# Layer norm sums beside the convolution: partial sums on POOL, a per-token shift as first summand, half the column sums on PE

## The chip, the cores and the metric

The kernel runs on one core of a Trainium2 chip. The metric is device time in microseconds (us) for one execution of the whole program. The core has five engines with their own instruction queues: PE (matmuls), DVE and POOL (elementwise vector work), ACT (activation functions, copies) and SP (here only the issue of DMAs). Each engine takes its instructions strictly in the order in which the program's scheduler put them.

## What is computed

One encoder block over 512 tokens of width 1024. The part that the change touches is the convolution branch and its neighbour, the attention:

```python
def conformer_conv(a_in, dw_w, dw_b, ln_g, ln_b, w_pw):
    u = a_in[..., :CONV_DIM] * jax.nn.sigmoid(a_in[..., CONV_DIM:])      # GLU
    u = lax.conv_general_dilated(u, dw_w[:, None, :], ...,               # 31 taps, one filter per channel
        feature_group_count=CONV_DIM) + dw_b
    u = layernorm(u, ln_g, ln_b)       # mean and variance over the 1024 channels of each token
    u = jax.nn.silu(u)
    return u @ w_pw
...
attn_out = windowed_gqa(q, k, v, attn_sink[l]) @ attn_w_o[l]             # 16 heads, band of 128 keys each way
merged = gates[:, :, 0, :] * conv_out + gates[:, :, 1, :] * attn_out     # sigmoid gates
x = x + merged @ w_out[l]
x = x + peer_ffn(rmsnorm(x, norm2_g[l]), ...)                            # 128 x 128 experts, 8 heads, top 16
```

The layer norm is (u - mean) * rsqrt(var + eps) * g + b over channels. Adding the same number to all channels of a token changes neither u - mean nor the variance.

## The kernel before

Activations are kept transposed: channels on the 128 partitions, 512 tokens along the free dimension, eight tiles of 128x512 for 1024 channels (`cv[:, k, :]`, k = 0 to 7). Every large matmul is done in three passes over split operands (`mm3`, L63 to L67): a value is split into a rounded part `hi` (ACT copy, L59) and the rest `lo` (a subtraction on POOL or DVE, L60). A projection (`proj`) of eight 128x128 weight chunks is therefore 24 matmuls of 512 columns; its weights come by DMA into `wraw`, are split in two halves (`whi` on ACT, `wlo` on the engine that `lo_engine` names), and there are four buffers of halves of each kind.

A scheduler lays out each engine's queue ahead of time: ready work goes in order of the program text, and work that stands later in the text fills an engine that has nothing earlier that is ready. Real durations don't change that order any more.

The stages around the change, in the order of the text:

1. **Convolution stage.** PE runs projections without a break: the GLU inputs (`glu`, two projections for each channel tile), keys, values, queries and 11 of the 16 gate projections (`fill`). Beside it DVE runs the 31 taps of the depthwise convolution (`conv`, L258 to L267) for pairs of channel tiles, the taps of the two tiles interleaved. The first tap of a tile is a `tensor_scalar` (L263) that writes the accumulator `ca` in PSUM with the bias `dwb` added; the other 30 are `scalar_tensor_tensor` (L266), and the last one writes `cv` in SBUF. A pair needs the GLU results `ub` (L255) of its two tiles. POOL makes `wlo` for all projections.
2. **Attention.** 16 blocks `attend(g, b)` for four key heads g and four query blocks b; the PSUM banks for its outputs (`pso`) are those that the convolution's accumulators held. ACT does the exponentials (L336, L338), half of the scaling (L344) and the copies `ph`, `qh` (L59); DVE the masked logits (L328), the other half and the rests `pl`, `ql` (L60). Five gate projections fill in between, each written by ACT into the gate tiles `sg` (L303).
3. **Layer norm.** Column sums over channels are matmuls with a matrix `ones` whose entries are 1/1024: eight of `cv` for the mean (L398), then, after DVE has subtracted the mean (L403) and ACT has squared (L405), eight of the squares for the variance (L406). These matmuls are of plain float32 and show as two passes of 512 columns each. Then ACT takes the square root (L408), DVE the reciprocal (L409), and per tile DVE multiplies (L411), ACT applies Silu (L413), and the result is split into `ac_hi`, `ac_lo` for the pointwise projection. These two take the buffers of the transposed input `hT`, whose last reader is the last gate projection.
4. **Output projections.** The two gates' sigmoids are two ACT instructions over 128x4096 (L421). Then eight projections with `w_o` (their `lo_engine` is DVE, L425), each result multiplied into the gate (L426), which frees the PSUM bank (there are two, `mm`); then eight with `w_pw`, then `w_out`. Weights of `w_out` are split with POOL (`olo`).
5. The expert stage, some three quarters of the time, which the change doesn't touch.

## Time and profile before

| | us |
|---|---|
| median of three runs | 1776.07 |
| lowest, highest | 1769.18, 1780.47 |
| the profiled execution | 1779.59 |
| its span on the core, first to last instruction | 1777.8 |

The profiled execution is 3.5 us above the median. The profile lists for each engine the time in which it was busy. Matmuls are pipelined and the listed durations of neighbours overlap, so a PE that is busy for the whole of a stretch may still be slower than its pace; the starts of successive matmuls show the pace. "[x <-E t Lnn]" at the end of a row of the timeline means that the engine had been idle for x us, and that the wait ended with engine E finishing a piece of work on tile t in line nn. PEclk is the share of full speed that TensorE's clock was granted.

### The profile page before, as it was taken

Reading aid. Unit: us, or ns where it says so; the run is one execution under the profiler, and the core shown is the slowest. Engines: PE = TensorE matmul, PEld = TensorE weight load, DVE = VectorE, ACT = ScalarE, POOL = GpSimd, SP = SyncE. Lnnn points to the kernel's source line nnn. Section 1 sums busy time; section 2 is a strip of 40 time slices with the busy share of each in tenths; the row PEclk is TensorE's granted clock in tenths of the full one; section 3 lists DMA queues with packets and bytes.
Section 4 is the critical chain, followed back from the end, with each engine's and each line's share of the span. In section 5 each row is a group of like instructions: output and inputs, shape, how many; then the busy total and the mean of one; then the engine's idle time right before and its main releaser. Section 6 shows DMA issues by size and latency. Waiting matters only on the chain.

```text
span 1777.8 us, 25338 instructions
## 1 busy us (share of the span) xinstructions
PE 1723.7 (97%) x8843; PEld 1487.6 (84%) x8843; DVE 1425.5 (80%) x2523; ACT 777.7 (44%) x1386; POOL 945.5 (53%) x745
## 2 busy tenths in 40 slices
PE   7999999989999979999999999999999999998998
PEld 6888876668888878998999999999999988997786
DVE  7999967674437999999668888888878768898964
ACT  5333368972253336665433333333433332332343
POOL 6544420020135444445358888878876677786401
PEclk9999999999999989999999999999999999999999
DMA  4232210043243125987879998988997888899952
GB/s 160 98 102 97 95 39 33 13 148 101 83 149 105 45 65 162 285 259 245 311 256 312 328 317 307 328 320 316 319 326 278 314 303 294 304 329 333 357 204 93
DMA packets 158976, 379.44 MB, mean 213 GB/s; under 512 B 12592, under 2 KB 64832, under 8 KB 158848
## 3 DMA queue, kind: packets, MB, share of 16 engines
q1 hardware_dynamic: 120720, 241.73, 38.9%
q0 software_dynamic: 37120, 134.52, 22.0%
q10 hardware_dynamic: 1008, 1.58, 0.3%
q8 instruction: 69, 1.13, 0.3%
q14 instruction: 59, 0.48, 0.1%
HBM read 346.84 MB, written 30.93 MB: 212 GB/s over the span
## 4 chain that ended last, share of the span: by engine, by line
PE 63%; DVE 13%; DMA 12%; issue 6%; POOL 3%; ACT 2%; SPq 0%; ACTq 0%; POOLq 0%; DVEq 0%
PE mm L65 7%; PE mm L67 7%; PE mm L66 7%; PE acc L67 6%; PE acc L66 6%; PE acc L65 6%; PE hps L66 6%; PE hps L65 6%; PE hps L67 5%; DMA row<-in_v_dram,eidx 5%; DMA uraw<-in_ut_dram 3%; DMA vraw<-in_v_dram 2%; PE s L65 2%; POOL row L701 1%; PE s L66 1%
## 5 line engine op out<-in xcount | busy, mean ns | idle before, releaser
L60 POOL TENSOR_TENSOR ulo<-uraw,uhi 128x512 fp32r<-128x512 f32 x256 | 400.7, 1581 | 306.6 <-ACT uhi L59 278.7
L67 PE MATMUL hps<-big,ulo 128*128 128x384 f32 x1024 | 349.0, 341 | 3.6 <-POOL ulo L60 3.6
L65 PE MATMUL hps<-big,uhi 128*128 128x384 f32 x1024 | 348.8, 341 | 2.2 <-ACT hb L504 2.1
L66 PE MATMUL hps<-big,uhi 128*128 128x384 f32 x1024 | 347.5, 339 | 0.0
L67 PE MATMUL acc<-vhl,pl 128*128 128x512 f32 x768 | 301.7, 393 | 8.0 <-DVE pl L60 8.0
L65 PE MATMUL acc<-vhl,ph 128*128 128x512 f32 x768 | 301.3, 392 | 3.6 <-ACT vhl L59 3.5
L66 PE MATMUL acc<-vhl,ph 128*128 128x512 f32 x768 | 301.7, 393 | 0.9 <-DVE vhl L60 0.9
L60 POOL TENSOR_TENSOR wlo<-wraw,whi 128x512 fp32r<-128x512 f32 x120 | 160.8, 1344 | 176.4 <-ACT whi L59 153.6
L708 DVE SCALAR_TENSOR_TENSOR row<-row,h2tok 128x1024 f32<-128x1024 f32 x128 | 206.0, 1610 | 58.3 <-DMA row<-in_u_dram,eidx 56.5
L719 DVE SCALAR_TENSOR_TENSOR yacc<-row,dots,yacc 128x1024 f32<-128x1024 f32 x127 | 193.3, 1522 | 58.4 <-DMA row<-in_v_dram,eidx 58.2
L59 ACT ACTIVATE vhl<-vraw 128x1024 fp32r<-128x1024 f32 x128 | 135.5, 1059 | 230.5 <-DMA vraw<-in_v_dram 207.8
L59 ACT ACTIVATE uhi<-uraw 128x512 fp32r<-128x512 f32 x256 | 157.1, 631 | 167.0 <-PE hps L66 75.3
L65 PEld LDWEIGHTS hps<-big,uhi 128*128 128x128 f32 x1024 | 194.4, 190 | 6.4 <-ACT hb L504 2.4
L67 PEld LDWEIGHTS hps<-big,ulo 128*128 128x128 f32 x1024 | 194.3, 190 | 5.3 <-POOL ulo L60 5.3
L66 PEld LDWEIGHTS hps<-big,uhi 128*128 128x128 f32 x1024 | 194.9, 190 | 4.0
L701 POOL DMA_INDIRECT row<-in_u_dram,eidx x128 | 178.6, 1396 | 31.6 <-issue 25.8
L59 ACT ACTIVATE whi<-wraw 128x512 fp32r<-128x512 f32 x152 | 95.2, 631 | 209.9 <-PE mm L66 141.5
L701 POOL DMA_INDIRECT row<-in_v_dram,eidx x128 | 155.1, 1211 | 55.5 <-DVE yacc L719 31.1
L60 DVE TENSOR_TENSOR vhl<-vraw,vhl 128x1024 fp32r<-128x1024 f32 x128 | 162.7, 1271 | 24.4 <-ACT vhl L59 24.2
L67 PEld LDWEIGHTS acc<-vhl,pl 128*128 128x128 f32 x768 | 145.3, 189 | 41.4 <-DVE pl L60 10.5
L65 PE MATMUL mm<-big,whi 128*128 128x512 f32 x448 | 178.0, 397 | 0.4 <-DVE big L105 0.4
L66 PE MATMUL mm<-big,whi 128*128 128x512 f32 x448 | 176.4, 394 | 0.0
(243 smaller groups left out, 3073.3 us busy)
## 6 DMA issues: line engine op xcount, KB each, us to landing
uraw<-in_ut_dram SPq DMA_DIRECT2D x128, 512.0 KB
vraw<-in_v_dram SPq DMA_DIRECT2D x128, 512.0 KB
gates_dram<-st SPq DMA_DIRECT2D x12, 2048.0 KB
gt<-gates_dram SPq DMA_DIRECT2D x96, 256.0 KB
wraw<-in_w_in_dram SPq DMA_DIRECT2D x42, 512.0 KB
wraw<-in_w_query_dram SPq DMA_DIRECT2D x16, 512.0 KB
wraw<-in_w_o_dram SPq DMA_DIRECT2D x8, 512.0 KB
oraw<-in_w_out_dram SPq DMA_DIRECT2D x16, 256.0 KB
```

The source lines that it names most:

```text
L59: ACT.activation(hi, src, AF.Copy)
L60: lo_engine.tensor_tensor(lo, src, f(hi), op=OP.subtract)
L65: PE.matmul(ps, wh, mh, start=first and i == 0, stop=False)
L66: PE.matmul(ps, wh, ml, start=False, stop=False)
L67: PE.matmul(ps, wl, mh, start=False, stop=last and i == n - 1)
L701: POOL.indirect_dma_start(out=row, out_offset=None, in_=table, in_offset=bass.IndirectOffsetOnAxis(ap=eidx[:, c:c + 1], axis=0))
L708: DVE.scalar_tensor_tensor(row, row, 1.0, h2tok, op0=OP.mult, op1=OP.mult, accum_out=dots[:, c:c + 1])
L719: DVE.scalar_tensor_tensor(yacc, row, dots[:, c:c + 1], yacc, op0=OP.mult, op1=OP.add)
```

## The change

Three things. First, the sums over channels for tiles 0 to 5 are made by POOL while the convolution still runs: `ssum` collects the sum of the tiles, `sqsum` that of their squares, so that only one partial sum and the last two tiles go through PE. Second, to keep the squares small, all tiles carry a per-token shift: the mean of tiles 0 and 1 (`cshift`, two matmuls, one ACT copy). POOL subtracts it from these two tiles; for tiles 2 to 7 an ACT instruction makes `dwb` minus `cshift`, and the first tap adds it (now a `scalar_tensor_tensor` too). The unused planes of the gate tiles `sg` hold these arrays. The variance is the mean of the squares less the square of the mean. Third, the sums are finished after the first attention block (`ln_sums`: six matmuls, four ACT instructions, one DVE subtraction), the square root stands right behind the attention loop, and the eight squares and the second pass over the tiles are gone. The `lo` halves of the `w_o` weights move from DVE to POOL (`proj` has POOL as its default).

```diff
@@ conv @@
+            cshift, ssum = sg[0][:, 6, :], sg[0][:, 7, :]
+            sqt, sqsum = sg[1][:, 6, :], sg[1][:, 7, :]
+
             def conv(pair, ubs):
                 accs = [psc.tile([P, S], F32, name="ca") for _ in pair]
+                offs = []
+                for i in pair:
+                    if i > 1:
+                        offs.append(accs[1] if i % 2 else sg[0][:, 5, :])
+                        ACT.activation(offs[-1], cshift, AF.Identity, scale=-1.0, bias=vec["dwb"][:, i:i + 1])
                 for j in range(TAPS):
-                    for i, ub, acc in zip(pair, ubs, accs):
-                        if j == 0:
+                    for n, (i, ub, acc) in enumerate(zip(pair, ubs, accs)):
+                        if j == 0 and i < 2:
                             DVE.tensor_scalar(acc, ub[:, :S], tapt[:, i, 0:1], vec["dwb"][:, i:i + 1],
                                               op0=OP.mult, op1=OP.add)
                         else:
                             DVE.scalar_tensor_tensor(cv[:, i, :] if j == TAPS - 1 else acc, ub[:, j:j + S],
-                                                     tapt[:, i, j:j + 1], acc, op0=OP.mult, op1=OP.add)
+                                                     tapt[:, i, j:j + 1], acc if j else offs[n],
+                                                     op0=OP.mult, op1=OP.add)
+                if pair[0] == 0:
+                    ps = psm.tile([P, S], F32, name="mm")
+                    for i in pair:
+                        PE.matmul(ps, ones, cv[:, i, :], start=i == 0, stop=i == 1)
+                    ACT.activation(cshift, ps, AF.Copy, scale=float(KD // 2))
+                    for i in pair:
+                        POOL.tensor_tensor(cv[:, i, :], cv[:, i, :], cshift, op=OP.subtract)
+                if pair[0] < KD - 2:
+                    for i in pair:
+                        if i == 1:
+                            POOL.tensor_tensor(ssum, cv[:, 0, :], cv[:, 1, :], op=OP.add)
+                        elif i:
+                            POOL.tensor_tensor(ssum, ssum, cv[:, i, :], op=OP.add)
+                        sq = sqt if i else sqsum
+                        POOL.tensor_tensor(sq, cv[:, i, :], cv[:, i, :], op=OP.mult)
+                        if i:
+                            POOL.tensor_tensor(sqsum, sqsum, sq, op=OP.add)
@@ attention and layer norm @@
+            lnp = ac.enter_context(tc.tile_pool(name="lnp", bufs=2))
+            mu = lnp.tile([P, S], F32, name="mu", bufs=1)
+            rs = lnp.tile([P, S], F32, name="rs", bufs=1)
+
+            def ln_sums():
+                ps = pso.tile([P, S], F32, name="ln")
+                for n, a in enumerate((ssum, cv[:, KD - 2, :], cv[:, KD - 1, :])):
+                    PE.matmul(ps, ones, a, start=n == 0, stop=n == 2)
+                ACT.activation(mu, ps, AF.Copy)
+                ACT.activation(rs, mu, AF.Square)
+                ps = pso.tile([P, S], F32, name="ln")
+                for n in range(2):
+                    sq = lnp.tile([P, S], F32, name="act", bufs=2)
+                    ACT.activation(sq, cv[:, KD - 2 + n, :], AF.Square)
+                    PE.matmul(ps, ones, sq, start=n == 0, stop=False)
+                PE.matmul(ps, ones, sqsum, start=False, stop=True)
+                DVE.tensor_tensor(rs, ps, rs, op=OP.subtract)
+
             for g in range(4):
                 make_bias(g)
                 for b in range(NT):
                     attend(g, b)
+                    if (g, b) == (0, 0):
+                        ln_sums()
                     if b == 1 or (g, b) == (0, 3):
                         fill(1)
-            lnp = ac.enter_context(tc.tile_pool(name="lnp", bufs=2))
             ac_hi, ac_lo = bigtile(), bigtile()
-            mu_ps = pso.tile([P, S], F32, name="ln")
-            for k in range(KD):
-                PE.matmul(mu_ps, ones, cv[:, k, :], start=k == 0, stop=k == KD - 1)
-            mu = lnp.tile([P, S], F32, name="rs", bufs=1)
-            ACT.activation(mu, mu_ps, AF.Copy)
-            var = pso.tile([P, S], F32, name="ln")
+            ACT.activation(rs, rs, AF.Sqrt, bias=epst)
+            DVE.reciprocal(rs, rs)
             for k in range(KD):
                 DVE.tensor_tensor(cv[:, k, :], cv[:, k, :], mu, op=OP.subtract)
-                sq = lnp.tile([P, S], F32, name="sq")
-                ACT.activation(sq, cv[:, k, :], AF.Square)
-                PE.matmul(var, ones, sq, start=k == 0, stop=k == KD - 1)
-            rs = lnp.tile([P, S], F32, name="rs", bufs=1)
-            ACT.activation(rs, var, AF.Sqrt, bias=epst)
-            DVE.reciprocal(rs, rs)
-            for k in range(KD):
                 DVE.tensor_tensor(cv[:, k, :], cv[:, k, :], rs, op=OP.mult)
                 act = lnp.tile([P, S], F32, name="act", bufs=2)
                 ACT.activation(act, cv[:, k, :], AF.Silu, scale=vec["lng"][:, k:k + 1],
@@ output projection @@
             for j in range(KD):
-                ps = proj(w_o[j], oT, lo_engine=DVE)
+                ps = proj(w_o[j], oT)
                 DVE.tensor_tensor(sg[1][:, j, :], ps, sg[1][:, j, :], op=OP.mult)
```

## Rows read from the trace of the kernel before

**Rows 1.** Windows, three stages: from:to, length, PE, PEld, DVE, ACT, POOL, PEclk, DMA.

```profile
45.00:231.00 186.00, 186.00 (x826) 153.55 (x825) 179.77 (x275) 59.86 (x104) 92.09 (x78) 1.00 0.30 98
231.00:367.00 136.00, 133.35 (x622) 92.96 (x620) 92.79 (x289) 113.66 (x274) 7.74 (x6) 1.00 0.07 22
367.00:418.00 51.00, 46.55 (x178) 35.07 (x178) 29.73 (x42) 28.13 (x44) 10.58 (x8) 0.93 0.53 174
```

**Rows 2.** Timeline of PE, 362 to 394 us: start, us, engine, line, tiles [idle before].

```profile
362.19 1.88 PE L406 MATMUL ln<-sq,ones 128*128 128x512 f32 x4
...
365.28 3.73 PE L406 MATMUL ln<-sq,ones 128*128 128x512 f32 x8
368.45 0.80 PE L65 MATMUL mm<-qh,whi 128*128 128x512 f32 x1
...
377.78 0.51 PE L65 MATMUL mm<-qh,whi 128*128 128x512 f32 x1 [1.43 <-DVE sg L426]
...
386.40 0.77 PE L65 MATMUL mm<-qh,whi 128*128 128x512 f32 x1 [2.76 <-DVE sg L426]
```

**Rows 3.** Timeline of DVE, 365 to 385 us, same columns.

```profile
366.31 0.69 DVE L60 TENSOR_TENSOR ql<-o,qh 64x512 fp32r<-64x512 f32 x1
...
373.65 3.35 DVE L409 RECIPROCAL rs<-rs 128x512 f32<-128x512 f32 x1 [4.72 <-ACT rs L408]
...
377.64 6.20 DVE L411 TENSOR_TENSOR cv<-cv,rs 128x512 f32<-128x512 f32 x7
```

**Rows 4.** Groups of PE's instructions, 367.5 to 418 us: count | busy, mean ns.

```profile
L65 PE MATMUL mm<-qh,whi 128*128 128x512 f32 x56 | 23.9, 427 | 4.2 <-DVE sg L426 4.2
```

**Rows 5.** The tile ln: duration min/median/max ns, first and last start.

```profile
L398 PE MATMUL ln<-cv,ones x16: 590/592/697, 317.2 to 333.6; 128*128 128x512 f32 x16
```

**Rows 6.** Timeline of ACT in the attention, two places.

```profile
307.86 1.28 ACT L421 ACT_TABLE_LOAD   x1
309.15 3.62 ACT L421 ACTIVATE sg<-sg 128x4096 f32<-128x4096 f32 x1
...
313.81 1.28 ACT L336 ACT_TABLE_LOAD   x1
...
358.12 0.58 ACT L400 ACTIVATE rs<-ln 128x512 f32<-128x512 f32 x1
```

**Rows 7.** Windows, PE's matmuls into attention output o alone: from:to, length, PE, PEclk.

```profile
262.00:278.00 16.00, 4.51 (x15) 1.00 0.11 34
...
306.00:322.00 16.00, 2.88 (x10) 1.00 0.04 14
322.00:338.00 16.00, 4.84 (x12) 1.00 0.10 34
```

**Rows 8.** Groups of instructions, 231 to 367 us, ACT.

```profile
L405 ACT ACTIVATE sq<-cv 128x512 f32<-128x512 f32 x5 | 2.9, 630 | 0.3 <-PE ln L406 0.3
```

**Rows 9.** Groups of instructions, 45 to 231 us, POOL and DVE.

```profile
L60 POOL TENSOR_TENSOR wlo<-wraw,whi 128x512 fp32r<-128x512 f32 x69 | 90.0, 1307 | 89.7 <-ACT whi L59 88.1 <-PE s L67 1.4
...
L266 DVE SCALAR_TENSOR_TENSOR ca<-ub,tapt,ca 128x512 f32<-128x512 f32 x232 | 154.7, 755 | 0.0
...
L255 DVE TENSOR_TENSOR ub<-mm,sgm 128x512 f32<-128x512 f32 x3 | 2.1, 688 | 2.8 <-ACT sgm L250 2.8
```

**Rows 10.** Timelines of POOL and DVE at the end of the first pair.

```profile
88.81 1.30 POOL L60 TENSOR_TENSOR wlo<-wraw,whi 128x512 fp32r<-128x512 f32 x1 [1.41 <-ACT whi L59]
91.20 0.11 POOL L252 MEMSET ub<- 128x15 f32 x1 [1.10 <-DVE cv L266]
...
91.70 0.58 DVE L364 SCALAR_TENSOR_TENSOR dist<-dist 128x384 f32<-128x384 f32 x1
...
94.46 1.49 DVE L366 TENSOR_TENSOR dist<-dist,L 128x384 f32<-128x384 f32 x1
```

**Rows 11.** Groups of instructions, 28 to 46 us, POOL and DVE.

```profile
L60 POOL TENSOR_TENSOR big<-cv,big 128x512 fp32r<-128x512 f32 x4 | 6.9, 1729 | 1.3 <-ACT big L59 1.3
...
L271 DVE SCALAR_TENSOR_TENSOR cv<-cv,g,sg 128x512 f32<-128x512 f32 x8 | 9.3, 1186 | 0.0
```

## Prediction

> **What bounds the kernel now.** I read the windows by stage first: beside each stretch stand its length and, engine by engine, busy time and count [rows 1]. In the convolution stage PE issues 826 matmuls in 186 us, one per 0.225 us, without a gap, and DVE is busy for 179.8 us of 186: two engines are full. In the attention PE is busy for 133.4 of 136 us, but with only 622 matmuls, many of them short, so that is no pace; ACT has 113.7 us of work in 136, the most of the others. From 367 to 418 us PE should be limited by itself, with 168 matmuls of `w_o` (three passes of 56) [rows 4], and isn't: it issues 178 in 51 us at a mean clock of 0.93 [rows 1].
>
> Why, PE's timeline shows [rows 2]. The last attention output is split when DVE ends `ql`, 366.31 + 0.69 = 367.0 us [rows 3]. But the variance's column sums hold PE until 368.45; four more of their passes follow among the projections (16 in all, as for the mean [rows 5], of which twelve stand in the two rows [rows 2]). Then PE idles 1.43 and 2.76 us for L426, the multiplication on DVE that frees the PSUM bank [rows 2]. DVE is late because the reciprocal (3.35 us, itself waiting 4.72 us for ACT's root) and seven multiplications (6.20 us) stand ahead of it [rows 3]. After the second gap the clock is granted at half: a mean of 0.93 over 51 us is 51 x 0.07 x 2 = 7.1 us at the lower level (1.2 instead of 2.4 GHz), which costs 3.6 us.
>
> **Tail: what is taken away.** Squares, their sums and the root's wait leave this stretch, and DVE is free for L426 at once. Term by term: 368.45 - 367.0 = 1.45; four passes at 1.88 / 4 = 0.47, less overlap 0.43, 1.7; the two gaps 4.2; the clock 3.6. Together -10.9 us. From the other end: 168 x 0.225 = 37.8 us from 367.0 is 404.8, against the end of the window that just holds them, 418 [rows 4]: -13. I take -10.9, with bounds -7 (one gap and its clock loss stay) and -13. The `lo` halves of `w_o` go to POOL at 1.31 instead of about 0.69 us on DVE: 2.6 us per projection of 24 x 0.225 = 5.4 us, beside the eight `olo`, and POOL is busy for 10.6 of 51 us there [rows 1, 9]; counted at nothing, as POOL has that room.
>
> **Convolution stage: what is added.** PE gets four passes, 4 x 0.43 = 1.7 us, in a stage where it has no gap. POOL gets six operations of 128x512 behind each of the first three pairs (two subtractions, one addition, two squares, one addition behind the first; two additions, two squares, two additions behind the others). At the 1.31 us of `wlo` that is 7.9 us in a row, and by the text they go before the `wlo` of the following projections, which POOL works off with half its time idle [rows 9]. How much lead has `wlo`? Four buffers of halves, 12 matmuls of 0.225 = 2.7 us for each: a half is begun when PE frees the one four back, so PE comes to it three halves (8.1 us) and two matmuls (0.45) later; ACT's copy (0.63, as for its other 128x512 work [rows 8]) and POOL's 1.30 [rows 10] leave 6.6 us. A row of 7.9 us makes one half late by 1.3 us and stalls PE by that. The two bursts near 92 and 142 us count, since the last GLU inputs come from PE behind them and DVE waits for such inputs already (up to 2.8 us [rows 9]); what PE loses there the last pair, and the attention behind it, gets later. So 1.7 + 2 x 1.3 = +4.3 us. Bounds: +1.7 if the scheduler puts `wlo` in between; +11.8 if POOL's operations take the 1.73 us that they take beside DVE work [rows 11], 2 x (10.4 - 6.6) = 7.6, and POOL stands 2.5 us for `cshift` with `wlo` behind it. The skew of the laid-out order is small: POOL's waits for the end of a pair are 1.10 us [rows 10].
>
> The new chain, last tap to sum (0.86) to ACT copy to ACT offset (0.63 each) to first tap, is about 2.5 us with its handovers; DVE has the distance tables (0.58, 1.49 [rows 10]) and a query split to do meanwhile, so nothing; uncovered 2.5 us. Later offsets are made while the other tile's tap runs: nothing, at most 0.6 us for each pair. Do POOL's added operations slow DVE? A tap takes 0.755 us on average over 232 with POOL busy for half the time [rows 9]: one input is in PSUM. The multiplication L271, with both inputs in SBUF, took 1.19 us on average beside POOL's `big` splits, and those 1.73 instead of 1.31 [rows 9, 11]. The Trainium skill says the same ("SBUF — State Buffer", Who interferes with whom): a DVE instruction with two SBUF inputs and a POOL instruction that reads SBUF exclude each other. By it the three first taps that read their offset from SBUF could each be held for one POOL operation, 3 x 1.3 = 3.9 us more. I count nothing for the taps.
>
> **Attention: what moves in.** ACT gets four instructions of 0.63 in `ln_sums` (2.5 us), and the root, which was behind the attention, can now run in the first gap of ACT after the first block. So can Silu for two tiles (two buffers `act`; the split that frees them needs `hT`'s buffers, which the last gate projection holds). What such an insertion costs the rows show for the sigmoids: each came into the attention with a table load before and one behind it, 1.28 each, 6.2 us with its 3.62 [rows 6]. The stretches of 16 us that hold them have 10 and 12 matmuls into `o` where an undisturbed one has 15 [rows 7]: 5.3 and 3.2 us of progress lost for 12.4 us of ACT, or 0.69. Root: 0.63 + 2 x 1.28 = 3.2. A pair of Silu: 1.3 + 2.6 = 3.9. Leaving: the mean's copy (0.58 [rows 6]) and five squares (2.9 [rows 8]). Net 2.5 + 3.2 + 3.9 - 3.5 = 6.1 us on ACT, times 0.69: +4.2 us. The reciprocal (3.35) and sixteen short DVE operations go into the 43 us that DVE has idle here [rows 1]; without that cover up to 3.4. PE's mean sums (16 passes [rows 5]) leave, twelve passes come: 1.7 us of filler less, nothing. Bounds: -2.4 (only the leaving counts) to +23 (below).
>
> The Trainium skill speaks against this order ("ScalarE: Activation LUTs", Table sets: the hidden batching unit): do all work of one table set before the next. It puts a switch at 2.66 us, load and drain; the sum with that for the four switches would be 4 x 1.38 x 0.69 = 3.8 us higher, 1778 us. The rows show the sigmoid starting 1.29 us behind its load's start [rows 6], no drain beyond, so the sum stays with 1.28.
>
> **Sum.** 4.3 + 4.2 - 10.9 = -2.4 us. The profiled execution, 1779.59 us, would become 1777.2; from the median, 3.5 us below it, 1776.07 - 2.4 = 1773.7. I forecast 1774 us: a real gain of 11 us at the tail, mostly spent ahead of it. 1% is 17.8 us, about what a measurement of this kernel can tell from no change.
>
> **Rivals.** *Clean gain.* The bursts slip between `wlo` (+1.7), the attention takes the insertions in gaps (-2.4), the tail gives 13: -13.7, 1762 us; if Silu pushes the second sigmoid behind the attention, 3.2 to 5.3 us more, 1757 to 1759. For it: ACT has 22 us idle in the attention; DVE sheds `wlo`. The mean's copy, ready when its sums ended near 334 us, ran only at 358.12 [rows 5, 6], so late work may simply stay late, and then adds no switches. Against: both sigmoids did get in.
>
> *Silu scattered through the attention (slower).* Place: ACT's gaps between exponentials, as soon as buffers allow. Eight single Silu with two loads each: 8 x (0.63 + 2.56) = 25.5; root 3.2, sums 2.5, eight `hi` copies 5.0, less 3.5: 32.7 us on ACT, times 0.69 is 22.6. With 4.3 - 10.9: +16, 1792 us; passed on in full, +26, 1802. It turns the gain into a loss when ACT gets 6.6 / 0.69 = 9.6 us, which is one more switch than I count, and passes 1% at 35. For it: the text puts Silu ahead of the sigmoids. Against: `hT` holds the buffers for six of them until the last gate projection, and ACT is 84% full (113.7 of 136).
>
> *POOL becomes the gate of the weights.* The upper bound of the convolution stage, +11.8, with the rest as summed: +5, 1781 us. For it: POOL then has 92 + 18 x 1.31 = 116 us of work in bursts. Against: half its time is idle.
>
> **How the numbers follow.** Forecast (1765 to 1783 us): 0.47. Clean gain: 0.29, about half of it beyond 1%. Scattered Silu: 0.14, most of it beyond 1%. POOL as gate: 0.10. So faster by over 1%: 0.15; slower by over 1%: 0.11; within: 0.74. The range leaves out the far ends of the clean gain and the full price of the scattered Silu: 1759 to 1790 us.
>
> **What would show it.** Tail: no column sums after 365 us, `w_o`'s 168 matmuls in 38 to 40 us, granted clock 1.00 there. Convolution: last tap 2 to 8 us later; six POOL operations in a row behind a pair, then a stall of PE of 1 to 2 us. Attention: two to four more table loads, stretch from last tap to last `ql` about 141 instead of 137 us. It is wrong if that stretch shortens, if loads number eight or more, or if PE stalls by over 5 us at a burst.

## The result, and the profile after

The changed kernel takes 1828.19 us (median of 4 runs, 1823.75 to 1839.05), the kernel before 1772.87 (4 runs, beside it): 1.031 times as long, 95% interval 1.027 to 1.035. That is +55.3 us where I had forecast -2.4; the time lies 38 us above the upper end of my range.

The waits of the changed kernel, 25 to 300 us (engine, line, tile, releaser: us in total, times, longest), name the place by the longest single waits (rows left out are marked):

```profile
...
ACT whi L59 <- PE mm L66: 56.8, 27, 2.2
PEld mm L280 <- DVE cv L274: 50.8, 2, 50.3
PE mm L280 <- DVE cv L274: 49.8, 1, 49.8
ACT sg L281 <- PE mm L280: 44.7, 1, 44.7
...
POOL ub L252 <- DVE cv L274: 39.7, 2, 39.2
...
```

And PE's timeline there (start, us; what idle time came before stands in brackets):

```profile
34.99 0.40 PE L66 MATMUL s<-ql,whi 128*128 128x512 f32 x1
35.23 0.40 PE L67 MATMUL s<-qh,wlo 128*128 128x512 f32 x1
85.45 3.78 PE L280 MATMUL mm<-cv,ones 128*128 128x512 f32 x4 [49.83 <-DVE cv L274]
...
89.46 0.63 PE L66 MATMUL mm<-ql,whi 128*128 128x512 f32 x1
89.89 0.63 PE L67 MATMUL mm<-qh,wlo 128*128 128x512 f32 x1
90.31 0.55 PE L65 MATMUL mm<-qh,whi 128*128 128x512 f32 x1
90.70 0.39 PE L66 MATMUL mm<-ql,whi 128*128 128x512 f32 x1
90.93 0.39 PE L67 MATMUL mm<-qh,wlo 128*128 128x512 f32 x1
```

L280 is the shift's column sum over the first two convolved tiles. It stands in PE's queue directly behind the second GLU projection (35 us), but its input, the last tap of the first pair, comes 50 us later. PE takes the queue as it stands: not one matmul ran in 49.83 us. The windows by stage (from:to, length; PE, PEld, DVE, ACT and POOL with counts; clock, DMA share, GB/s), against [rows 1]:

```profile
45.00:90.00 45.00, 4.54 (x7) 2.30 (x8) 41.06 (x63) 0.69 (x2) 1.61 (x6) 0.50 0.00 0
90.00:274.00 184.00, 184.00 (x814) 152.00 (x813) 144.51 (x209) 62.16 (x106) 106.73 (x88) 1.00 0.29 92
274.00:433.00 159.00, 149.58 (x646) 104.84 (x646) 105.20 (x303) 125.51 (x291) 14.15 (x11) 0.92 0.07 21
433.00:478.00 45.00, 43.78 (x187) 34.67 (x186) 9.57 (x13) 22.26 (x34) 29.52 (x23) 1.00 0.66 218
```

Seven matmuls in the first 45 us, where 826 in 186 us make some 200. Then 814 matmuls in 184 us, the old pace, to the last tap at 273.9 us; DVE, which was full before, is now busy for 144.5 of 184 us. The attention is longer too, and PE's clock in it 0.92. Only the tail shows what was forecast for it: 1.00 and no gaps to speak of, as the groups of `w_o`, 433 to 478 us, say against [rows 4]:

```profile
L67 PE MATMUL mm<-qh,wlo 128*128 128x512 f32 x62 | 24.6, 397 | 0.7 <-POOL wlo L60 0.7
L65 PE MATMUL mm<-qh,whi 128*128 128x512 f32 x62 | 24.6, 397 | 0.5 <-ACT whi L59 0.5
```

The table that carries the rest of this text has the milestones of every kernel run, read from the traces, in us: the end of the first pair's first tile on DVE, of the last tap, and of the last split `ql` of the attention; the stretch between the latter two; the start of `w_pw`, and the tail up to it; and how many matmuls of `w_o` were left when the attention ended. The experiments are described below.

| kernel | first tile | last tap | attention ends | stretch | `w_pw` starts | tail | left | ratio to before [interval] |
|---|---|---|---|---|---|---|---|---|
| before | 91.1 | 230.3 | 367.0 | 136.7 | 417.8 | 50.8 | 168 | |
| changed | 85.4 | 273.9 | 432.5 | 158.6 | 477.9 | 45.4 | 186 | 1.0306 [1.0267, 1.0345] |
| e1 sum in another bank | 92.1 | 233.8 | 384.3 | 150.5 | 428.9 | 44.6 | 185 | 1.0051 [1.0031, 1.0072] |
| e2 the sum alone | 85.5 | 273.1 | 422.0 | 148.9 | 474.4 | 52.4 | 168 | one run: 1830.6 |
| e3 `lo` on POOL alone | 90.8 | 230.0 | 369.7 | 139.7 | 422.4 | 52.7 | 168 | one run: 1777.5 |
| e4 no shift | 91.3 | 230.5 | 380.3 | 149.8 | 425.5 | 45.2 | 186 | one run: 1785.4 |
| e5 = e1, root held | 91.0 | 232.7 | 376.3 | 143.6 | 424.9 | 48.5 | 166 | 1.0046 [1.0020, 1.0073] |
| e6 = e5, `lo` on DVE | 91.0 | 232.7 | 376.3 | 143.6 | 422.6 | 46.3 | 166 | 1.0038 [1.0013, 1.0062] |
| e7 = e6, no shift | 92.2 | 231.9 | 376.3 | 144.4 | 422.4 | 46.1 | 166 | 1.0007 [0.9981, 1.0032] |
| e8 = e6, sums late | 90.7 | 232.3 | 369.1 | 136.8 | 415.8 | 46.7 | 167 | 0.9984 [0.9962, 1.0005] |
| e10 = e8, mult. on POOL | 90.8 | 232.5 | 370.8 | 138.3 | 417.0 | 46.2 | 167 | 0.9961 [0.9943, 0.9979] |
| e9 = e10, no shift | 92.6 | 232.2 | 368.9 | 136.7 | 415.1 | 46.2 | 167 | 0.9966 [0.9944, 0.9988] |
| e11 = e10, sums kept | 91.4 | 233.1 | 373.4 | 140.3 | 415.4 | 42.0 | 166 | 0.9985 [0.9965, 1.0005] |
| e12 = e11, no shift | 91.2 | 230.4 | 370.0 | 139.6 | 412.1 | 42.1 | 166 | 0.9951 [0.9933, 0.9968] |

From `w_pw` to the first matmul into `hps` (the next stage) all of them take 90 us; from there to the last matmul into `acc` 1250.6 to 1266.1 us, with no relation to the edits (before 1261.9, changed 1252.3). Each row of milestones is one execution, which can lie off its kernel's median (e1's by 13 us); the ratios are of medians, against runs of the kernel before in the same group (medians 1771.1 to 1776.1). The milestones up to `w_pw` therefore say more about the change than the last digit of the times; that the changed kernel is 60.1 us late at `w_pw` and 55.3 at the end is within this spread.

### The profile page after: what moved, and what is told of

It is laid out like the page before. It is cut to its first block, busy times and chain, and to the rows that moved or that the text cites. A ratio compares the mean times of both kernels' runs of the same rounds, so it can differ in the third digit from the quotient of the medians.

```text
span 1828.6 us, 25332 instructions
## 1 busy us (share of the span) xinstructions
PE 1725.1 (94%) x8827; PEld 1487.1 (81%) x8827; DVE 1422.1 (78%) x2508; ACT 788.4 (43%) x1393; POOL 975.2 (53%) x779
## 4 chain that ended last, share of the span: by engine, by line
PE 73%; DVE 13%; issue 7%; DMA 4%; POOL 1%; ACT 1%; ACTq 0%; POOLq 0%; SPq 0%; DVEq 0%
PE acc L66 8%; PE acc L67 8%; PE acc L65 8%; PE hps L65 8%; PE hps L66 8%; PE hps L67 8%; PE mm L65 6%; PE mm L66 6%; PE mm L67 6%; DVE ca L274 2%; DMA row<-in_v_dram,eidx 2%; DVE oij L707 1%; DVE ohl L709 1%; PE s L65 1%; POOL row L735 1%
## 5 line engine op out<-in xcount | busy, mean ns | idle before, releaser
L60 POOL TENSOR_TENSOR wlo<-wraw,whi 128x512 fp32r<-128x512 f32 x136 | 181.1, 1338 | 270.3 <-ACT whi L59 245.1
L742 DVE SCALAR_TENSOR_TENSOR row<-row,h2tok 128x1024 f32<-128x1024 f32 x128 | 188.4, 1472 | 59.8 <-DMA row<-in_u_dram,eidx 58.6
L753 DVE SCALAR_TENSOR_TENSOR yacc<-row,dots,yacc 128x1024 f32<-128x1024 f32 x127 | 187.1, 1474 | 44.4 <-DMA row<-in_v_dram,eidx 43.8
L59 ACT ACTIVATE ph<-hb 128x384 fp32r<-128x384 f32 (+1 forms) x132 | 67.3, 513 | 289.8 <-PE acc L66 282.6
L59 ACT ACTIVATE whi<-wraw 128x512 fp32r<-128x512 f32 x152 | 95.1, 629 | 208.9 <-PE mm L66 129.6
L735 POOL DMA_INDIRECT row<-in_u_dram,eidx x128 | 167.3, 1307 | 31.7 <-issue 25.6
L60 DVE TENSOR_TENSOR vhl<-vraw,vhl 128x1024 fp32r<-128x1024 f32 x128 | 158.7, 1240 | 26.1 <-ACT vhl L59 25.9
```

The lines of the kernel that those rows point to most:

```text
L59: ACT.activation(hi, src, AF.Copy)
L60: lo_engine.tensor_tensor(lo, src, f(hi), op=OP.subtract)
L735: POOL.indirect_dma_start(out=row, out_offset=None, in_=table, in_offset=bass.IndirectOffsetOnAxis(ap=eidx[:, c:c + 1], axis=0))
L742: DVE.scalar_tensor_tensor(row, row, 1.0, h2tok, op0=OP.mult, op1=OP.mult, accum_out=dots[:, c:c + 1])
L753: DVE.scalar_tensor_tensor(yacc, row, dots[:, c:c + 1], yacc, op0=OP.mult, op1=OP.add)
```

## The experiments

**The wait: e1 and e2.** Theory: the 50 us come from the column sum's PSUM tile. It is taken from the pool of `mm`, whose two banks serve all projections but the GLU inputs of the odd tiles (tile `s`); the tile framework gives them out in the order of the text, so each later projection comes behind L280 in PE's queue. Rival: the wait is the chain's own, or POOL's bursts behind it. e1 takes the tile from the convolution's pool and changes nothing else; e2 puts only the sum and its copy into the kernel before.

```
e1 (changed kernel):
-                    ps = psm.tile([P, S], F32, name="mm")
+                    ps = psc.tile([P, S], F32, name="ca")
e2 (kernel before, behind the taps):
+                if pair[0] == 0:
+                    ps = psm.tile([P, S], F32, name="mm")
+                    for i in pair:
+                        PE.matmul(ps, ones, cv[:, i, :], start=i == 0, stop=i == 1)
+                    ACT.activation(sg[0][:, 6, :], ps, AF.Copy, scale=float(KD // 2))
```

> The changed kernel with one edit: the PSUM tile of the shift's column sums (two matmuls over tiles 0 and 1) comes from the convolution's own two banks instead of the two banks that all projections share. Theory A (banks are handed out in the order of the text, so every projection that stands behind the sums waits for the first pair's last tap): PE's gap of 50 us at 35 us goes, the last tap falls at 234 to 238 us instead of 273.9, and the time is 1828 - 39 = about 1789 us, since the attention still is about 20 us longer than before. Theory B (the new chain and POOL's bursts hold DVE and PE whatever the bank): PE still idles 30 us or more in the first 100 us and the time stays above 1815 us.

> The kernel before, plus only the two column sum matmuls over tiles 0 and 1 and the ACT copy of the result, in a bank of the projections; nothing reads the result. Theory A: PE idles about 45 to 50 us behind the second GLU projection pair, last tap near 270 us instead of 230.3, time 1810 to 1820 us. Theory B: four passes more, 1773 to 1777 us.

Measured: e1 1782.25 us (7 under what I expected), last tap 233.8; e2 1830.6 us in its one run, last tap 273.1, and its waits, 25 to 300 us, have the same row as the changed kernel's:

```profile
PE mm L271 <- DVE cv L266: 49.3, 1, 49.3
ACT sg L272 <- PE mm L271: 44.3, 1, 44.3
```

In e1 the four passes ran at 92.19 us with no idle time before them:

```profile
92.19 1.99 PE L280 MATMUL ca<-cv,ones 128*128 128x512 f32 x4
```

So the choice of the pool is worth 46 us, and two matmuls alone make the kernel as slow as the whole change does. In the changed kernel 48 matmuls into `mm` follow L280 and then 48 into `s`, in the order of the kernel before; that those into `s`, with banks of their own, waited too is the queue's order, and why the scheduler put them there no run isolates. e2 was some 10 us slower than I expected, because I had not followed the delay: at the attention's end it is 55.0 us late. 49.3 of that is the wait, 1.7 the passes; PE then ran at the lower clock level for a while, which in the changed kernel lost 2.6 us (from 85.45 to 90.70 us, 5.25 us, for work that takes 4 x 0.43 + 4 x 0.23 = 2.65). DVE's taps for the first pair ran on during the wait, and the last tap is only 42.8 us late; the other 12.2 us come back in the attention, whose scores stand behind PE's remaining projections. A lead that one engine keeps is paid back where the engines meet.

**Root and Silu: e5.** e1 is still 17.3 us late at the attention's end. Its ACT rows, 234 to 384 us, count the table loads (before a function of another set ACT loads that set's table):

```profile
L362 ACT ACT_TABLE_LOAD x6 | 7.7, 1283 | 0.1
L447 ACT ACTIVATE act<-cv,lnb,lng 128x512 f32<-128x512 f32 x7 | 5.7, 815 | 0.1
...
L447 ACT ACT_TABLE_LOAD x4 | 5.1, 1283 | 0.1
...
L441 ACT ACT_TABLE_LOAD x1 | 1.3, 1283 | 0.0
L455 ACT ACT_TABLE_LOAD x1 | 1.3, 1283 | 0.0
```

L447 is Silu: three times singly, with a load ahead and one (L362, exponential) behind it, between 266 and 353 us, and four times behind one load at 376 us. e5 makes the root's bias from the last element of the attention's last output, which keeps root and Silu behind the attention.

```
-            ACT.activation(rs, rs, AF.Sqrt, bias=epst)
+            epl = lnp.tile([P, 1], F32, name="epl", bufs=1)
+            DVE.tensor_scalar(epl, f(ql[:, KD - 1, S - 1:]), 0.0, EPS, op0=OP.mult, op1=OP.add)
+            ACT.activation(rs, rs, AF.Sqrt, bias=epl)
```

> As the run with the sums in the convolution's bank, and the square root takes its bias from a 128x1 tile that DVE makes from the last attention output, so that root, reciprocal, multiplications and Silu can't start in the attention. Theory C (the attention is 20 us longer because root and Silu came into it, each with table loads on ACT): the stretch from the last tap to the last ql goes from 158.6 back to 136 to 141 us, table loads in it from eleven to five, time about 1789 - 20 = 1769 us. Theory D (it is longer for another reason: the six column sums at its start, less work for PE to fill with, the clock): the stretch stays above 150 us and the time above 1782 us.

Measured: 1780.5 us; stretch 143.6 us, 6.9 less than e1 and with the five loads of before, but not within the 136 to 141 us that I expected; and the tail 4 us longer, though 19 matmuls fewer were left for it, so that the time (1769 expected) can't be told from e1's. The first part of the theory holds, and something else lengthens the attention. In the tail PE stood 7.8 us, at 387 us, behind the multiplication L462 on DVE, the same wait as before the change [rows 2], moved.

**The low part of `w_o`: e3.** The kernel before, with these subtractions on POOL as in the change (`proj(w_o[j], oT)`), nothing else.

> The kernel before with only the lo halves of the w_o weights on POOL. If DVE's backlog is what holds the projections behind the attention, the half that came 0.06 us before its use is early again, one small wait (0.3 us) goes, and L426 is a little earlier: 1768 to 1773 us. If POOL (with the w_out splits) becomes late instead: PE waits for wlo and the time is 1776 to 1782 us.

`w_pw` starts at 422.4 us, 4.7 later (stretch +3.0, tail +1.9); the time, in one run, is within what runs differ by. I had counted this part at nothing. In the tail the waits that grew are not those for `wlo` but those for L426: 7.0 us instead of 4.2. Ahead of it in DVE's queue stand the multiplications by the reciprocal root, with both inputs in SBUF. Their times (least, median, longest ns; first and last start) in the kernel before and in e3, then in e6 and e5 (below), which also differ by the low part alone:

```profile
L411 DVE TENSOR_TENSOR cv<-cv,rs x8: 679/680/1779, 377.6 to 385.0; 128x512 f32<-128x512 f32 x8
L411 DVE TENSOR_TENSOR cv<-cv,rs x8: 676/1424/1784, 380.8 to 391.0; 128x512 f32<-128x512 f32 x8
L447 DVE TENSOR_TENSOR cv<-cv,rs x8: 677/1178/1783, 381.6 to 390.1; 128x512 f32<-128x512 f32 x8
L447 DVE TENSOR_TENSOR cv<-cv,rs x8: 679/1752/1783, 381.7 to 392.9; 128x512 f32<-128x512 f32 x8
```

Those that overlap no subtraction on POOL take 0.68 us, those that lie wholly beside POOL's subtractions 1.7 to 1.8 us, and POOL's then take 1.7 us instead of 1.3. With the low part on POOL more of them do. Seven took 9.09 us in e3 and 6.20 before [rows 3]. That covers the tail's 1.9 us; the 3.0 us in the attention stay open.

**The shift, first look: e4.** The changed kernel without it (all tiles start from the bias, no subtraction).

> The changed kernel without the shift: no column sums of the first pair, no offsets, no subtractions, all taps start from the bias as before; the sums for the layer norm stay on POOL and ln_sums, the root and the Silu stay as changed (the variance then comes from unshifted sums). Theory (the 50 us come from the shift's sums alone, the rest of the change costs the convolution only its POOL bursts): PE has no stall near 35 us, the last tap ends at 231 to 232.5 us (230.3 before, 233.8 with the shift whose sums stand in the convolution's bank), so the shift's own work is worth 1.5 to 3 us; the attention stretch stays at about 148 to 152 us, since the scattered root and Silu are still in it; time about 1778 to 1782. Rival (POOL's squares and sums, not the shift, delay the weights): the last tap stays at 233 us or later, time 1782 or more.

The last tap comes at 230.5 us (I had given 231 to 232.5), as before the change (230.3), with all of POOL's sums and squares in place. The attention stays long (149.8), and the time is 1785.4 us: my expectation of 1778 to 1782 was too good by 3 us; the stages up to `w_pw` moved as expected (3.4 us ahead of e1).

**What is left in the attention: e6 and e7.** e6 is e5 with the low part of `w_o` back on DVE, e7 the same without the shift.

> As e5_root_held (sums in the convolution's bank, root and Silu held until the attention is over), and the low part of w_o back on DVE as before the change. Theory A (root and Silu in the attention, and then w_o's low part on POOL, made the stretch longer; the 8 us hole of PE in e5's tail stood behind DVE's multiplications): stretch 139.5 to 141.5 us (143.6 with the low part on POOL, 136.7 before), tail 42 to 46 us, w_pw starts at 415 to 420 us, time 1771 to 1776. Rival B (the sums at the attention's start take the fillers that PE needs later, whoever makes the low part): stretch stays at 143 to 145 us, time 1777 to 1782.

> As e6_root_held_lo_on_dve without the shift (the variance comes from unshifted sums). Theory A: last tap 231 to 232 us, stretch 139.5 to 141.5 us, tail 42 to 46 us, w_pw starts at 413 to 418 us, time 1768 to 1774, at or just below the kernel before: the layer norm's sums beside the convolution are worth what they free in the tail less what the attention pays. Rival B: stretch 143 to 145 us, time 1775 to 1780.

Measured: 1778.62 and 1775.89 us. The stretch did not move (143.6, 144.4): rival B's numbers came, not my theory's. The trace says where the loss lies. Each of the attention's 16 blocks ends with a `ql` on DVE; I call them head parts. The third ends at 271.89 + 0.68 in e6, at 265.05 + 0.68 before:

```profile
271.89 0.68 DVE L60 TENSOR_TENSOR ql<-o,qh 64x512 fp32r<-64x512 f32 x1 [0.47 <-ACT qh L59]
265.05 0.68 DVE L60 TENSOR_TENSOR ql<-o,qh 64x512 fp32r<-64x512 f32 x1
```

Ahead of it PE made the twelve passes of `ln_sums` (tile `ln` in e6: durations, first and last start):

```profile
L421 PE MATMUL ln<-cv,ones x4: 592/592/697, 238.5 to 239.9; 128*128 128x512 f32 x4
L428 PE MATMUL ln<-act,ones x4: 592/592/697, 244.8 to 246.2; 128*128 128x512 f32 x4
L421 PE MATMUL ln<-sg,ones x2: 590/590/591, 236.6 to 237.0; 128*128 128x512 f32 x2
L429 PE MATMUL ln<-sg,ones x2: 592/594/595, 247.5 to 247.9; 128*128 128x512 f32 x2
```

And PE has no room there: of 231 to 262 us it is busy throughout in e6,

```profile
231.00:246.00 15.00, 15.00 (x59) 9.83 (x58) 7.65 (x29) 8.26 (x20) 2.73 (x3) 1.00 0.22 71
246.00:262.00 16.00, 16.00 (x76) 11.30 (x75) 14.06 (x40) 10.95 (x29) 1.30 (x1) 1.00 0.00 0
```

as it was in the kernel before, where the same 16 us held ten matmuls more and ACT was busy for 4 us more:

```profile
246.00:262.00 16.00, 16.00 (x86) 12.44 (x85) 11.56 (x36) 14.88 (x42) 0.00 (x0) 1.00 0.00 1
```

Twelve passes at 0.43 (the distance of their starts in e1) are 5.2 us, placed ahead of the heads. Before the change the mean's passes stood at 317 to 334 us [rows 5]. PE shows no gap there either, with these passes among its work (kernel before):

```profile
310.00:326.00 16.00, 16.00 (x74) 10.39 (x73) 7.50 (x25) 14.28 (x31) 0.00 (x0) 1.00 0.01 2
326.00:342.00 16.00, 16.00 (x73) 10.90 (x72) 11.62 (x42) 13.85 (x23) 0.00 (x0) 1.00 0.10 34
```

So a full window doesn't tell by itself what passes cost in it; e8, which moves them, does.

e6's tail: the stall was 5.2 us now (7.8 in e5, whose eight multiplications took 11.88 us), and DVE's timeline shows what stands ahead of the second L462:

```profile
381.00 0.69 DVE L462 TENSOR_TENSOR sg<-mm,sg 128x512 f32<-128x512 f32 x1
381.61 9.18 DVE L447 TENSOR_TENSOR cv<-cv,rs 128x512 f32<-128x512 f32 x8
390.72 1.28 DVE L60 TENSOR_TENSOR big<-act,big 128x512 fp32r<-128x512 f32 x2
391.92 1.28 DVE L462 TENSOR_TENSOR sg<-mm,sg 128x512 f32<-128x512 f32 x2
```

**The sums late: e8, e10, e9.** e8 is e6 with `ln_sums()` called behind the loop over the heads; e10 has the eight multiplications L447 on POOL as well; e9 is e10 without the shift. In these three the gates of the last fillers overwrite the buffers of the running sums before `ln_sums` reads them, so the layer norm's values are not the reference's, and the second sigmoid has to wait for the sums.

```
-                    if (g, b) == (0, 0):
-                        ln_sums()
...
+            ln_sums()
             ac_hi, ac_lo = bigtile(), bigtile()
...
-                DVE.tensor_tensor(cv[:, k, :], cv[:, k, :], rs, op=OP.mult)
+                POOL.tensor_tensor(cv[:, k, :], cv[:, k, :], rs, op=OP.mult)    (e10, e9)
```

> As e6_root_held_lo_on_dve, and the layer norm's last sums (five column-sum matmuls, mu, its square, DVE's difference) written behind the attention instead of behind its first block, so that they fill PE's gaps at the attention's end as the sums did before the change. Theory (in the last three kernels the attention lost 5 us in its second and third head part, 252.5 to 272.6 us against 250.5 to 265.7 before, because the sums stand there ahead of the heads' own work): the third head part ends at 267 to 269 us, stretch 137 to 140.5 us (143.6), time 1771 to 1776 (1778.6). Rival (the head parts are slow there for another reason, the order of the weights' splits): the third part still ends at 271 us or later, stretch 142 to 145 us, time 1777 to 1781.

> As e8_sums_late, and the eight multiplications by the reciprocal root on POOL instead of DVE. Theory (the hole of 5.3 us in PE at 387 us of the e6 and e7 kernels is an eviction on DVE queued behind eight multiplications of 1.5 us each): no PE gap over 2 us after the attention, tail 42 to 44 us against 46 (e6), time 3 to 5 us under e8_sums_late, 1767 to 1772. Rival (POOL and DVE slow each other, or the Silu then comes too late for w_pw): tail 46 us or more, time as e8_sums_late or above.

> As e10_sums_late_mult_on_pool without the shift (the variance comes from unshifted sums). Theory: last tap 231 to 232 us, stretch 137 to 140 us, tail 42 to 44 us, w_pw starts at 411 to 415 us against 417.8 before, time 1765 to 1769, 0.2 to 0.4% under the kernel before. Rival (what leaves the tail is again paid in the attention): w_pw starts at 417 us or later, time 1771 or more.

e8: 1772.86 us; the third part ends at 265.81 + 0.68 us,

```profile
265.81 0.68 DVE L60 TENSOR_TENSOR ql<-o,qh 64x512 fp32r<-64x512 f32 x1
```

6.1 us earlier than in e6, and 0.5 earlier than I gave; that part of the theory holds. The stretch is 136.8 us, but not by the sums alone: the second sigmoid left the attention's middle for its end. e11, where it is back, will give a cleaner number. e10's multiplications on POOL did not shorten the tail (46.2 against 46.7; my 42 to 44 was wrong): PE's wait for DVE's multiplication, 2.4 us in e8, is gone, but its waits for `wlo` rose from 1.0 to 2.6 us. `w_pw` starts 1.2 us later; its ratio is lower than e8's, but the intervals overlap, so this part stays undecided. The second sigmoid now came at the attention's end, and PE stood for the last output's split behind it (e8, ACT, then PE):

```profile
362.85 1.28 ACT L456 ACT_TABLE_LOAD   x1
364.15 3.62 ACT L456 ACTIVATE sg<-sg 128x4096 f32<-128x4096 f32 x1
```

```profile
368.44 0.79 PE L65 MATMUL mm<-qh,whi 128*128 128x512 f32 x1 [3.35 <-ACT qh L59]
```

e9's `w_pw` at 415.1 and 1769.21 us lie just past the upper ends of its theory; its tail, 46.2, missed the 42 to 44 as well. Without the shift the time is no better than e10's.

**All repaired: e11 and e12.** As e10 and e9, with the two running sums copied by POOL to buffers of their own at the convolution's end, so that the sigmoids need not wait.

```
+            keep2 = lnp.tile([P, 2, S], F32, name="keep2", bufs=1)
+            POOL.tensor_copy(keep2[:, 0, :], ssum)
+            POOL.tensor_copy(keep2[:, 1, :], sqsum)
+            ssum, sqsum = keep2[:, 0, :], keep2[:, 1, :]
```

> As e10_sums_late_mult_on_pool, but the two running sums are first copied by POOL into buffers of their own at the convolution's end, so that the gates of the last fillers do not overwrite them (in the e8, e9 and e10 kernels they do: there the layer norm gets gate values for its sums, and the second sigmoid has to wait for the sums, which put it at 363 us, after the attention's last block). All parts of the change stand: the shift, the sums beside the convolution on POOL, half the column sums on PE. Theory (what the change cost was the bank, the early sums, the scattered root and Silu, w_o's low part on POOL and DVE's multiplications; all five are gone here): third head part at 266 to 268 us, stretch 135.5 to 138 us, tail 42 to 46 us, w_pw starts at 412 to 416 us (417.8 before), time 1765 to 1769, ratio 0.995 to 0.998. Rival (the shift and the copies cost as much as the tail gives): w_pw starts at 417 us or later, ratio 0.999 or more.

> As e11_sums_late_kept without the shift (the variance comes from unshifted sums). Theory (the shift's own work is 1 to 3 us in the convolution and nothing elsewhere): w_pw starts 0.5 to 3 us earlier than with the shift, time 1763 to 1768, ratio 0.993 to 0.997. Rival (the shift is free once its bank is harmless): the same as e11 within 0.1%.

e11, with every part of the change, 1772.43 us: no faster than before that could be told (0.9985, interval up to 1.0005). The third head part (267.3 us), the tail (42.0) and `w_pw` (415.4) came as expected; the stretch, 140.3, is longer than the 135.5 to 138 I wrote, and the time above my 1765 to 1769. Against e6, with both sigmoids in place again, the stretch is 3.3 us shorter: of the 5 to 6 us gained at the third part, somewhat more than half is left at the attention's end. The sums now stand at 320 to 342 us. e12 takes 1765.53 us, 0.9951 [0.9933, 0.9968]: the lowest median here, within its own theory, and faster than before by half a per cent. It is the change without its second part, the shift. Its three stages (compare [rows 1]):

```profile
45.00:230.00 185.00, 185.00 (x822) 152.76 (x821) 179.41 (x272) 59.36 (x103) 110.45 (x94) 1.00 0.30 97
230.00:370.00 140.00, 132.81 (x616) 93.26 (x615) 96.37 (x296) 113.50 (x273) 8.83 (x8) 0.98 0.08 27
370.00:412.00 42.00, 39.65 (x167) 31.01 (x167) 30.63 (x31) 24.93 (x40) 24.38 (x16) 1.00 0.56 199
```

The convolution is untouched although POOL does 18 us more work in it (110 against 92); the attention is 3 us longer, the tail 9 us shorter. The head parts run level with the kernel before down to the ninth (308.0 against 307.9 us). The twelfth is even 6.8 us ahead (335.5 against 342.3), the thirteenth, with the second sigmoid now ahead of it, 0.5 behind, and the fourteenth 4.3 behind: it takes 11.8 us instead of 8.0. These windows hold it, e12 first, then the kernel before:

```profile
350.00:362.00 12.00, 9.32 (x43) 7.14 (x43) 7.99 (x20) 11.07 (x31) 0.00 (x0) 0.82 0.13 44
350.00:358.00 8.00, 6.32 (x33) 4.05 (x31) 4.49 (x10) 7.85 (x22) 0.00 (x0) 1.00 0.00 0
```

In the six kernels whose granted clock stood at 1.00 there (before, e2, e3, e8, e9, e10) the fourteenth part takes 8.0 us, in the eight others, at half for a part of it, 9.9 to 12.8. In e12 it also holds ten matmuls more, and PE had idled 2.2 of the 16 us ahead of it. How much of the 3.8 us is the clock's, no run separates. Up to `w_pw` e12 is 5.7 us ahead of the kernel before, and 3.4 ahead of e11. That e12 is 6.9 us faster than e11 in the medians is more than the stages up to `w_pw` explain: of the 6.6 us between the two profiled executions 4.4 lie behind 1600 us, in the last stage, which differs by as much among kernels that are alike there.

## Why the prediction was wrong, step by step

**PE gets four passes: failed, and it is nearly the whole miss.** I priced the two matmuls by their length, 1.7 us, and the wait ahead of them only by what hangs on its result (the chain to the next first tap, 2.5 us). I didn't ask what stands behind them in PE's own queue. All later projections did: those into `mm` take their PSUM tiles from the same two banks and follow in the text, and those into `s` stand behind them. For POOL's wait for `cshift` I did count the `wlo` queued behind it; for PE I didn't. The rows held enough to see it: a pair has 62 taps of 0.755 us [rows 9], 46.8 us, that long PE works ahead of them without a gap [rows 1], and whatever waits for a pair's last tap at that place in its queue gives this lead away. The Trainium skill has the fact that decides ("TensorE: Matmul & The Clock Gate", The mechanism): matmuls start and end in program order, none overtakes another. The trace agrees: no matmul in 49.83 us. With the wait as measured, my sum would have come out at 1774 + 50 = 1824 us. That this is close to 1828 is partly luck, since the attention was mis-sized as well and part of that loss went under in the wait (below).

**The bursts on POOL: wrong in my favour.** I counted 2 x 1.3 us. Between the first tile's end and the last tap lie 139.2 us before; 139.2 to 139.7 in e4, e7, e9 and e12, which have the sums and squares on POOL but no shift; 141.6 to 141.7 in the six kernels that have both and a harmless bank. So the bursts cost 0 to 0.5 us. The squares were shorter than I took them, 1.04 us; the additions were not, 1.29. In the two later bursts the scheduler put one `wlo` in between, but the six operations behind the first pair ran in a row in e11 (95.1 to 102.7 us), longer than the 6.6 us of lead that I had worked out, and PE has no wait for `wlo` behind them: my lead was too small.

**The shift in a harmless bank: 1.9 to 2.5 us between the first tile and the last tap,** against 1.7 for its passes and nothing for the chain; the bound of the chain, another 2.5, was not reached. That the last tap came 3.5 us later in e1 (I said +4.3; 1.0 of it stands in the first tile's end already) is a fair sum of two wrong terms, so luck. In the times it shows only in part: e12 is 6.9 us under e11, e9 no better than e10.

**Attention: +4.2 forecast, +13.8 in e1.** Two terms, each shown by an edit. Root and Silu in the attention: 6.9 us of the stretch (e1 to e5), and 5.4 in the pair without the shift (e4 to e7). PE's clock is part of it: the mean granted over 233 to 376 us is 0.90 in e1 and 0.96 in e5. That is the rival of the scattered Silu, half way: three single Silu and four together instead of eight single ones, and twelve loads in place of five, although one sigmoid had gone behind the attention; I had forecast two to four loads more. My price of 0.69 per us of ACT took 15 matmuls into `o` as undisturbed [rows 7]; the windows 246 to 262 and 338 to 354 us have 22 and 18, so it was at the low end. The Trainium skill ("ScalarE: Activation LUTs", Table sets: the hidden batching unit) asks for all work of one set together; e5 followed it, and the trace agrees with a stretch shorter by 6.9 us. The Trainium skill's 2.66 us for a switch ("ScalarE: Activation LUTs", What ACT_TABLE_LOAD costs) are a load and a drain; the trace agrees on the load, 1.283 us, and shows no idle time for the drain (0.1 us ahead of four loads). The second term is `ln_sums`: I set its twelve passes off against the 16 that leave, and counted nothing. The place counts, not the number. Those that came stand at the attention's start, where PE is full (16.00 of 16 us): 5.2 us of PE, 5 to 6 us at the third head part, 3.3 us at the attention's end (e6 to e11). What the 16 had cost where they stood, in windows just as full, no run isolates. Together 10.2 of the 13.8; the rest, 3.6 us, is still there in e11, and there it arises behind the twelfth head part, as in e12. I had read PE's 133.4 of 136 us as a mean over the stage and not looked at which part of it has no gap.

**Tail: nearly right.** I forecast -10.9 us on 168 matmuls, 39.9 us. The changed kernel has 186 left at the attention's end, 18 more; 45.4 - 18 x 0.225 = 41.3 us, -9.5 on like terms, with the clock at 1.00 and no column sums, as I said that it would show. But the 18 come from the attention, which had done them before. With the low part on DVE and the sums late the tail is 42.0 us for 166 (e11).

**The low part of `w_o` on POOL: counted at nothing, 2.3 us (e5 to e6) to 4.7 (e3)** up to `w_pw`. I had looked only at POOL's busy time in that stretch. What it costs in the tail is DVE's: its multiplications with both inputs in SBUF and POOL's subtractions hold each other up (median 1.75 us in e5, 1.18 in e6), the effect that I had read from L271 [rows 11] and weighed for the taps, where it didn't show. The changed kernel's own tail paid none of it, since its multiplications ran in the attention, eight in 5.5 us.

**How the parts add up.** Up to `w_pw` the changed kernel is 60.1 us late. The sum alone makes 56.6 (e2); the change with its sum in a harmless bank 11.2 (e1). Together that would be 67.8: behind the wait the last tap is 43.6 us late with the whole change and 42.8 with the sum alone, so what the shift else costs found cover there, and the later, longer attention may have paid for part of its extra work in gaps that were there anyway. I didn't take that overlap apart further, so this is argued, not shown.

## What to carry to other kernels

Where an edit adds an instruction that waits long, read on which engine's queue it stands and what the text puts behind it there, buffers and banks first: here a small matmul that took a tile from a shared PSUM pool held every later taker of that pool, and so the engine. Price moved work by the place where it arrives and what stands behind it there, not by the mean of the stage; a window that is full tells that there is no gap, not what a pass costs. Before moving work to an idle engine, look at what runs beside it on the other one, and where the inputs of both lie. And set the text's order so that work of other table sets stays behind the loop that it would interrupt; tying the root's bias to the loop's last output was enough here.

## What the runs showed of the hardware

While PE stood, its clock was granted at half: 0.50 over 45 to 90 us, 1.2 of 2.4 GHz. The matmuls that followed started 0.42 us apart at 89.9 us and 0.23 apart from 90.7 on; the wait's aftermath cost 2.6 us, small beside the wait. POOL took on 18 us of additions and squares beside a DVE that was busy for 179.4 of 185 us (e12), and from the first tile to the last tap it took 139.2 us, as before (one input of a tap is in PSUM). A DVE multiplication with both inputs in SBUF, though, took 0.68 us with POOL idle and up to 1.78 us beside POOL's subtractions (e3, e5, e6 and the kernel before).
